# A two-layer decoder on one core: a gating unit's v product as one seven-product scheme, its layer norm's g and b moved behind the token mixing, and four weight residuals by accumulating transfers

## The chip, the cores and the metric

The kernel runs on one core of a Trainium2 chip. A core has engines with an instruction queue each: TensorE (PE in the profile; its weight loads are PEld), VectorE (DVE), ScalarE (ACT), GpSimd (POOL) and SyncE (SP), which here only issues transfers. They share an on-chip memory of 128 partitions and wait for each other by semaphores; matmul results stand in PSUM, in banks of 128 x 512 float32. The metric is the device time of one execution in microseconds, the median of several runs.

## The reference

x is 512 tokens of D = 1024 float32 values, and there are two layers. Each layer has a mixer and an MLP, each behind an RMS norm whose output is modulated by columns of `silu(c) @ ada_w` (48 columns of 128 for each layer, called modulation columns here). Layer 0's mixer is a pooling one, layer 1's is the gating unit that this change is about.

```python
h = modulate(rmsnorm(x, norm_mix_g[i]), sh1, sc1)
x = x + g1 * mixer(h)                       # i = 0: pooling; i = 1: sgu_mixer
h = modulate(rmsnorm(x, norm_mlp_g[i]), sh2, sc2)
x = x + g2 * (square(relu(h @ w1)) @ w2)    # D -> 4096 -> D

def sgu_mixer(h, w_in, ln_g, ln_b, w_s, b_s, w_out):
    z = gelu(h @ w_in)                      # 1024 -> 2048, exact gelu
    u, v = split(z, 2, axis=-1)
    v = layernorm(v, ln_g, ln_b)            # over 1024 features, eps 1e-5
    v = v.reshape(B, 4, 128, 8, 128)        # 4 chunks of 128 tokens, 8 heads of 128
    ws = where(tril(128, 128), w_s, 0)      # w_s: 8 x 128 x 128
    mixed = einsum('hts,bnshc->bnthc', ws, v) + b_s.T[None, None, :, :, None]
    return (u * mixed.reshape(B, 512, 1024)) @ w_out
```

## The kernel before

**Products in parts.** Every float32 operand of a product is split into a high part that TensorE takes in one pass and a residual: a weight tile `raw` gives `wh` (a copy by ACT) and `wl` (raw minus wh, by DVE), activations give `hb`/`op`/`as`/`gt` in the same two parts. A product is then three matmuls into one bank, wl x high, wh x residual and wh x high (`mm3`). `split` does this for a 128 x 1024 weight tile:

```python
A.activation(h[:, c], r[:, c], AF.Copy)
V.tensor_tensor(l[:, c], r[:, c], f32(h[:, c]), ALU.subtract)
```

**Stages, by time in the profiled execution.** Start, pooling mixer and the first sweep of MLP 0 to about 87 us; the rest of MLP 0 to 361; the gating unit from 361.4 to about 490; MLP 1 to about 797; the last norm and the store. Both MLP matrices already go through a seven-product scheme (Strassen's, in Winograd's form: block sums of weights and operands, seven block products for eight). Sums of weight blocks (`bt`, `tr`, `yr`) are partly made by transfers that accumulate into a tile, issued by POOL.

**Gating unit.** v has token rows on the partitions: for two halves of its columns (`ch`) and two halves of the tokens (`hf`), 8 feature blocks by 2 token tiles by 3 matmuls of 512 columns, then `Gelu` out of PSUM. `normed` meanwhile makes the second token half of h. The layer norm takes mean and variance of each token tile on DVE, the power for 1/sqrt on POOL (`rr<-rv`), scales v (`v<-v,ag,rr`), and applies `lnt`, which holds g and b for all partitions, by two DVE operations (`v<-v,lnt`). u is made with features on the partitions, 8 blocks `u0` to `u7` of 8 feature blocks x 3 matmuls. A mix `m0` to `m7` (one head) is 4 matmuls of v against the masked, transposed w_s in `wb[:, 0]`; DVE adds the bias in `wb[:, 1]` (`po<-po,wsbs`), multiplies by u (`u<-po,u`), ACT copies the high part and DVE makes the residual (`gt<-u,gt`). This one line orders u blocks and mixes:

```python
for op in "u0 u1 u2 u3 m0 u4 m1 m2 u5 m3 m4 u6 m5 u7 m6 m7".split():
```

The output projection takes `gt` against w_o in two column halves (`dh`) of four weight tiles each, four token tiles each; the first three token tiles take the heads 0 to 5 first and 6 and 7 afterwards. `gated` adds the result to x.

**Buffers.** PSUM is two pools of four banks: `xz` (v, mixes, projection) and `ps` (u, transposes, MLP parts). Weight parts `wh`/`wl` have five pairs. Three `raw` buffers of 128 x 1024 (pool `w4`) hold both raw weights and the modulation columns' tiles `ada`, each of which takes one DVE operation (`ada<-ada,cb`). `gq` has eight buffers of 128 x 2048 (tag g); `hx` holds single large tiles. `shift(pool, n)` puts an unused pad of n bytes a partition ahead of a pool's next tiles.

**Order.** The code after `plan.on = True` does not issue instructions: `Plan` records them and a list scheduler orders them for each engine, by a table of costs, by latest times counted back from PE's order, and by `yields`, by which DVE and ACT leave work that is not urgent for later. PE's order is that of the code. All instructions so issued bear line 128; code ahead of it bears line 100.

## Time and profile before

| | |
|---|---|
| time, median of 3 runs | 804.65 us (803.54 to 805.01) |
| profiled execution: its own time / span | 807.26 us / 805.2 us |
| granted TensorE clock, mean over the span | 0.997 |
| PE busy / PEld busy | 786.2 us (98%) / 712.0 us (88%) |
| DVE / ACT / POOL busy | 685.8 us (85%) / 504.9 us (63%) / 83.6 us (10%) |
| transfers | 183.35 MB, mean 228 GB/s |
| share of the chain that ended last | PE 79%, DMA 9%, DVE 5%, issue 4%, ACT 2% |

A row of groups reads "line engine operation out<-in partitions x elements xcount | busy us, mean ns of one | idle us before them, and what ended it". A row of the timeline reads "start, duration, engine, line, operation" and in brackets a wait and its releaser. A window's row has its length, the busy time of each engine with the instructions in it, the granted clock, the share of the transfer engines and GB/s. Matmuls overlap one another, so one's duration is longer than its share of TensorE's time, which is read from the distance of starts.

### The profile page before, as it was taken

The numbers are of one execution on the slowest core, as the hardware profiler recorded it, in microseconds if no ns is written. First come the engines' busy times: TensorE is split into PE (matmuls) and PEld (weight loads), VectorE is DVE, ScalarE is ACT, GpSimd is POOL, SyncE is SP. The second block draws the span as 40 slices with busy tenths as digits, with TensorE's granted clock in tenths as the row PEclk, the third lists the DMA queues.
The fourth block names the chain that finished last, engine by engine and source line by source line (L and its number), as shares of the span: only waits on it lengthen the run. The fifth ranks groups of instructions, "written<-read, shape, count | busy, mean of one in ns | idle before, by whom it ended". The sixth has DMA issues, their size and how long they took to land.

```text
span 805.2 us, 12574 instructions
## 1 busy us (share of the span) xinstructions
PE 786.2 (98%) x4868; PEld 712.0 (88%) x4868; DVE 685.8 (85%) x888; ACT 504.9 (63%) x718; POOL 83.6 (10%) x110
## 2 busy tenths in 40 slices
PE   5999999999999999999999999999999999999996
PEld 5678889999988888888889889999999998888885
DVE  5989799999789997986798878888778678998896
ACT  5486687777766666866234236777767685666672
POOL 4000001000010131010020002010000011112100
PEclk9999999999999999999999999999999999999998
DMA  8988958897999999244745756378776789999802
GB/s 342 417 303 298 358 195 286 272 281 209 312 291 241 232 242 257 95 161 140 256 154 205 260 195 213 143 199 241 228 235 172 183 261 272 199 230 208 216 14 91
DMA packets 46955, 183.35 MB, mean 228 GB/s; under 512 B 5272, under 2 KB 5424, under 8 KB 42928
## 3 DMA queue, kind: packets, MB, share of 16 engines
q1 hardware_dynamic: 36432, 129.33, 43.9%
q0 software_dynamic: 10032, 50.87, 30.5%
q10 hardware_dynamic: 432, 2.36, 0.7%
q8 instruction: 38, 0.62, 0.3%
q14 instruction: 21, 0.17, 0.1%
HBM read 176.23 MB, written 6.30 MB: 227 GB/s over the span
## 4 chain that ended last, share of the span: by engine, by line
PE 79%; DMA 9%; DVE 5%; issue 4%; ACT 2%; SPq 0%; POOLq 0%; POOL 0%; DVEq 0%; ACTq 0%
PE po L128 40%; PE pm L128 36%; DMA ada<-in_ada 3%; DMA raw<-in_w 1%; DMA wh<-in_ada 1%; DVE wl L128 1%; DMA bt<-in_w 1%; DMA x<-in_xtok 1%; ACT wh L128 1%; DVE ada L100 1%; PE po L100 1%; DMA yr<-in_w1b 1%; DMA tr<-in_w1b 1%; PE pq L100 0%; PE px L128 0%
## 5 line engine op out<-in xcount | busy, mean ns | idle before, releaser
L128 PE MATMUL pm<-wh,op 128*128 128x512 f32 x896 | 267.5, 379 | 0.0
L128 PE MATMUL po<-hb,wh 128*128 128x256 f32 (+1 forms) x1104 | 211.3, 295 | 0.0
L128 PEld LDWEIGHTS pm<-wh,op 128*128 128x128 f32 x896 | 169.4, 189 | 24.0
L128 PEld LDWEIGHTS po<-hb,wh 128*128 128x128 f32 x1104 | 174.2, 191 | 5.5
L128 PE MATMUL pm<-wl,op 128*128 128x512 f32 x448 | 169.9, 379 | 0.4 <-DVE wl L128 0.4
L128 PE MATMUL po<-hb,wl 128*128 128x256 f32 (+1 forms) x553 | 160.9, 296 | 0.9 <-ACT g L128 0.9
L128 PEld LDWEIGHTS po<-hb,wl 128*128 128x128 f32 x553 | 104.6, 191 | 4.1 <-ACT g L128 1.1
L128 PE MATMUL po<-as,wh 128*128 128x256 f32 x576 | 97.2, 275 | 0.0
L128 ACT ACTIVATE op<-g 128x1024 fp32r<-128x1024 f32 x56 | 59.1, 1061 | 58.5 <-PE pm L128 46.3
L128 PEld LDWEIGHTS pm<-wl,op 128*128 128x128 f32 x448 | 84.7, 189 | 12.5 <-DVE wl L128 0.7
L128 DVE TENSOR_TENSOR op<-g,op 128x1024 fp32r<-128x1024 f32 x56 | 68.1, 1220 | 24.0 <-ACT op L128 24.0
L128 PEld LDWEIGHTS po<-as,wh 128*128 128x128 f32 x576 | 87.4, 192 | 0.0
L128 DVE TENSOR_TENSOR wl<-bt,wh 128x1024 fp32r<-128x1024 f32 x64 | 76.8, 1217 | 7.1 <-ACT wh L128 7.1
L128 PE MATMUL po<-as,wl 128*128 128x256 f32 x288 | 79.3, 275 | 0.6 <-ACT g L128 0.6
L128 ACT ACTIVATE wh<-bt 128x1024 fp32r<-128x1024 f32 x64 | 67.4, 1053 | 19.8 <-PE pm L128 14.9
L128 ACT ACTIVATE wh<-tr 128x1024 fp32r<-128x1024 f32 x48 | 50.9, 1060 | 36.3 <-PE po L128 17.5
L128 DVE TENSOR_TENSOR wl<-raw,wh 128x1024 fp32r<-128x1024 f32 (+1 forms) x52 | 60.6, 1176 | 14.4 <-ACT wh L128 14.4
L128 DVE SCALAR_TENSOR_TENSOR ada<-ada,cb 128x1024 f32<-128x1024 f32 x56 | 67.9, 1217 | 5.1 <-DMA ada<-in_ada 5.1
L128 ACT ACTIVATE g<-g 128x512 f32<-128x512 f32 x100 | 61.8, 628 | 16.3 <-DVE g L128 15.1
L128 ACT ACTIVATE wh<-raw 128x1024 fp32r<-128x1024 f32 (+1 forms) x52 | 51.6, 1004 | 28.5 <-PE po L128 11.9
L128 DVE TENSOR_TENSOR wl<-tr,wh 128x1024 fp32r<-128x1024 f32 x48 | 58.6, 1221 | 10.8 <-ACT wh L128 10.7
L128 PEld LDWEIGHTS po<-as,wl 128*128 128x128 f32 x288 | 55.3, 192 | 0.8 <-ACT g L128 0.8
(192 smaller groups left out, 1135.1 us busy)
## 6 DMA issues: line engine op xcount, KB each, us to landing
ada<-in_ada SPq DMA_DIRECT2D x76, 512.0 KB, 4.9
bt<-in_w POOLq DMA_DIRECT2D x22, 1024.0 KB, 9.7
yr<-in_w1b SPq DMA_DIRECT2D x22, 512.0 KB, 6.4
bt<-in_w SPq DMA_DIRECT2D x16, 512.0 KB, 7.6
b<-in_w SPq DMA_DIRECT2D x16, 512.0 KB, 9.7
raw<-in_w SPq DMA_DIRECT2D x13, 512.0 KB, 6.8
tr<-in_w1b SPq DMA_DIRECT2D x12, 512.0 KB, 6.8
raw<-in_w1b SPq DMA_DIRECT2D x12, 512.0 KB, 5.3
```

The source lines that it names most:

```text
L100: return f(*a, **kw)
L128: self.ops.append((name, attr, lambda: f(*a, **kw), out, ins, kw))
```

## The change

**v's product.** The h @ w_v product is cut into 2 x 2 x 2 blocks (256 tokens, 512 features, 512 columns) and made as seven products v1 to v7, each 4 feature blocks x 2 token tiles x 3 matmuls of 512 columns. Partial sums that several results share stay in PSUM (`VX`, `VZ`); others go to v by ACT (copies) and are joined there by DVE (`v<-v,po`). Operand sums are made on DVE from a float32 copy of h (`hq`, which `normed` now fills in place of the scratch tile `tt`) and split again (`hs`). Weight sums are built in one tile `vb`: POOL issues 1 MB transfers that accumulate a further block into it, after the splits of the product before have read it.

```diff
+    CHAIN_ = {5: (0, 1), 6: (1, 1), 4: (1, 0)}
+    def h_sum(m):
+        if m == 5:
+            V.tensor_tensor(ha(1, 1), ha(1, 0), ha(1, 1), ALU.subtract)
+            t_[7] = get_gb().rearrange("p (k c) -> p k c", k=4)
+            V.tensor_tensor(t_[7], ha(0, 0), ha(1, 0), ALU.subtract)
...
+    def v_prep(m):
...
+        w = [split_d(b[q], src and wv_at(*src, q)) if f"v{m}{q}" in LO else split(b[q]) for q in range(2)]
+        if m in (1, 5, 6):
+            G.dma_start(whole_(VB[0, 0, 0]), wv_at(*CHAIN_[{1: 5, 5: 6, 6: 4}[m]]), accum_op=ALU.add)
+        if m == 5:
+            v_load(1, 1)
+        elif m == 3:
+            v_load(0, 1)
+            G.dma_start(whole_(VB[0, 1, 0]), wv_at(1, 1), accum_op=ALU.add)
...
+    def v_run(m, w):
+        banks = VX if m in (1, 6, 7, 4) else VS if m == 2 else VZ
...
+            if m in (1, 5) or m in (6, 3) and "v" not in half_:
+                A.activation(o, po, AF.Copy, scale=-1.0 if m == 6 else 1.0)
...
+            if m in (2, 3):
+                V.tensor_tensor(o, o, po, ALU.add)
+            elif m in (7, 6):
+                V.tensor_tensor(o, o, po, ALU.subtract)
+            A.activation(o, po if m == 4 else o, AF.Gelu)
```

**g and b.** v is only centred and scaled. g is a factor of a mix's row, applied together with the bias by one operation; b times the masked row sums of w_s is added to the bias table once. The row sums take a mask on POOL, a reduction on DVE, a transpose on PE and two transfers by POOL, out to memory and back to all partitions.

```diff
-        for n, op in ((0, ALU.mult), (1, ALU.add)):
-            V.tensor_tensor(v, v, lnt[:, n].rearrange("p (a b) -> p a b", a=2), op)
+    def rows():
...
+        G.affine_select(out=w, in_=w, compare_op=ALU.is_ge, fill=0.0, base=0, pattern=[[0, HEADS], [-1, P]], channel_multiplier=1)
+        V.tensor_reduce(rs, w, mybir.AxisListType.X, ALU.add)
+    def spread_rows(rs):
...
+        G.dma_start(line, r)
+        G.dma_start(b, line.rearrange("(o k) p -> o (k p)", o=1).to_broadcast([P, D]))
+        for h in range(HEADS):
+            V.scalar_tensor_tensor(wb[:, 1, h], b[:, P * h : P * h + P], vec[:, V_LNB + h : V_LNB + h + 1], wb[:, 1, h], ALU.mult, ALU.add)
     def do_mix(hd):
-        V.tensor_tensor(p4, p4, wb[:, 1, hd, :].unsqueeze(1).to_broadcast([P, 4, P]), ALU.add)
+        V.scalar_tensor_tensor(p4, p4, vec[:, V_LNG + hd : V_LNG + hd + 1], wb[:, 1, hd, :].unsqueeze(1).to_broadcast([P, 4, P]), ALU.mult, ALU.add)
```

**Residuals by transfers.** For u5, u7 and the third and fourth weight tile of the projection's first half, `wl` is no DVE subtraction: ACT writes minus the high part, and POOL issues a transfer that adds the raw weights from memory.

```diff
+    LO = "u5 u7 o2 o3".split()
+    def split_d(r, src=None):
+        h, l = wpair()
+        A.activation(h, r, AF.Copy)
+        A.activation(l, r, AF.Copy, scale=-1.0)
+        G.dma_start(l, r if src is None else src, accum_op=ALU.add)
```

**Order.** One line orders all of it: v products, u blocks (u0 and u1 in token halves, so that they can start before the second half of h is there), mixes `m`, their gates `g` (product with u and the parts), norms `n`, and modulation columns `c`. Each product's weights are prepared one product ahead.

```diff
-    for op in "u0 u1 u2 u3 m0 u4 m1 m2 u5 m3 m4 u6 m5 u7 m6 m7".split():
+    SEQ = "v1 v2 u0a u1a r0 u0b v5 u1b c2 u2 v6 c2 v3 c2 r1 v7 c2 u3 c1 n0 n1 v4 c1 n2 n3 c1 u4 c1 u5 m0 u6 m1 m2 c1 m3 g0 g1 u7 m4 g2 s0 g3 m5 m6 m7 g4 g5 g6 g7".split()
-    shift(hx, BASE)
+    shift(vy, BASE)
+        lock = {i for i, o in enumerate(ops) if o[0] == "POOL" and o[1] == "tensor_tensor"}
+        gap = {i for i in lock if any(ops[j][0] == "DVE" for j in succs[i])}
```

In the planner, `lock` lets POOL's element operations (the powers) be placed only where DVE is free, and `gap`, of 2.0 us, holds DVE back shortly before such a power that DVE awaits. A pad moves from the pool `hx` to the pool `vy`, which shifts the places of the tiles allotted behind it.

POOL's queue in the gating unit, before (-) and after (+); `rr<-sums` are the powers of RMS norms and `rr<-rv` those of v's norm:

```order
 L128 DMA x_1266<-xd_930 128x2048
-L128 TENSOR_TENSOR rr<-sums,mhalf 128x1 x3
+L128 AFFINE_SELECT ada<-ada 128x1024
+L128 TENSOR_TENSOR rr<-sums,mhalf 128x1 x2
+L128 DMA vb<-in_w_v 128x2x1024
 L128 AFFINE_SELECT wsbs<-wsbs 128x1024
-L128 TENSOR_TENSOR rr<-sums,mhalf 128x1
+L128 TENSOR_TENSOR rr<-sums,mhalf 128x1 x2
+L128 DMA vb<-in_w_v 128x2x1024 x3
+L128 DMA rowsum<-line 8x128
+L128 DMA ada<-rowsum 128x1024
+L128 DMA wl<-in_w_u 128x1024
```

Ahead of the second mask now stands the mask of the row sums, and between the norms' powers stand four 1 MB issues, the row sums' two and the first residual transfer.

VectorE before, from m6's bias to the last residual and the columns behind it, where the projection begins:

```order
L128 TENSOR_TENSOR po<-po,wsbs 128x512
L128 SCALAR_TENSOR_TENSOR ada,pmv<-ada,cb 128x1024
L128 TENSOR_TENSOR u<-po,u 128x512
L128 TENSOR_TENSOR po<-po,wsbs 128x512
L128 SCALAR_TENSOR_TENSOR ada,pmv<-ada,cb 128x1024
L128 TENSOR_TENSOR u<-po,u 128x512
L128 TENSOR_TENSOR gt<-u,gt 128x512
L128 SCALAR_TENSOR_TENSOR ada,pmv<-ada,cb 128x1024
L128 TENSOR_TENSOR gt<-u,gt 128x512
L128 SCALAR_TENSOR_TENSOR ada,pmv<-ada,cb 128x1024 x2
```

Here biases, products with u and columns stand in turn. VectorE after, from m4's bias on; the products with u in it are those of heads 4, 5, 6 and 7:

```order
L128 SCALAR_TENSOR_TENSOR po<-po,vec,wsbs 128x512
L128 TENSOR_TENSOR gt<-u,gt 128x512
L128 TENSOR_TENSOR u<-po,u 128x512
L128 SCALAR_TENSOR_TENSOR po<-po,vec,wsbs 128x512
L128 TENSOR_TENSOR gt<-u,gt 128x512
L128 TENSOR_TENSOR u<-po,u 128x512
L128 TENSOR_TENSOR gt<-u,gt 128x512 x3
L128 SCALAR_TENSOR_TENSOR ada,pmv<-ada,cb 128x1024 x3
L128 SCALAR_TENSOR_TENSOR po<-po,vec,wsbs 128x512 x2
L128 TENSOR_TENSOR u<-po,u 128x512
L128 TENSOR_TENSOR mods_90<-pmv,vec 128x2
L128 TENSOR_TENSOR u<-po,u 128x512
```

Three columns now stand between the residual of head 5 and the biases of m6 and m7. On PE, u7 stands ahead of m4, and m5, m6 and m7 follow each other with the projection right behind them.

More of the change, by code (lines that the diff above doesn't have):

```diff
@@ L332, in run @@
                 for e in ready:
+                    if e == "DVE" and any(i in gap and when[i] <= now + 1e-9 and k - cost[i][1] < now + lead["gap"] for k, i in ready["POOL"]):
+                        continue
                     if free[e] > now + 1e-9 or e == "SP" and sum(x[0] for x in lines[e]) > self.QUEUED or len(lines[e]) > 6:
@@ L340, in run @@
                             k, i = heapq.heappop(ready[e])
-                            if when[i] <= now + 1e-9 and fits(i) and not (e in ("DVE", "ACT") and yields(e, i)):
+                            if when[i] <= now + 1e-9 and fits(i) and not (e in ("DVE", "ACT") and yields(e, i)) and not (i in lock and free["DVE"] > now + 1e-9):
                                 pick = i
@@ L369, in run @@
                         end = now + cost[i][1]
+                        if i in gap:
+                            free["DVE"] = now + cost[i][0]
                         heapq.heappush(events, (end, i))
@@ new lines, in decoder_kernel, with u_prep, u_run @@
+    wu, pu = {}, {}
+    def u_prep(n):
+        r = ur[:, n % 2]
+        Y.dma_start(r, w_u[n])
+        w = split_d(r, w_u[n]) if f"u{n}" in LO else split(r)
+        return [t.rearrange("p (k c) -> p k c", k=KD) for t in w]
+    def u_run(n, w, part=None):
+        if n not in pu:
+            pu[n] = bank("po")
+        po = pu[n]
+        c = ALL if part is None else slice(256 * part, 256 * part + 256)
+        for k in range(KD):
+            mm3(po[:, c], cut(w, ALL, k), apart(H(k, c)), k == 0, k == KD - 1)
+        if part == 0:
+            return
+        if n % 4 == 0 and n // 4 == len(us):
+            us.append(gq.tile([P, 4, S], F32, name="u", tag="g"))
+        x = us[n // 4][:, n % 4]
+        if part is None:
+            A.activation(in_row(x), in_turn(po), AF.Gelu)
+        else:
+            x, po = x.rearrange("p (r c) -> p r c", r=2), po.rearrange("p (r c) -> p r c", r=2)
+            A.activation(in_row(x), in_turn(po), AF.Gelu)
@@ L1585, in decoder_kernel @@
+    ex = cols
     h_[0] = hparts()
```

226 lines of the change are left out of this document (160 added, 66 removed).

## Prediction

> **What bounds the kernel now.** I read the busy times first, then the chain that ended last, then the gating unit's stretch by sub-stages.
>
> ```profile
> PE 786.2 (98%) x4868; PEld 712.0 (88%) x4868; DVE 685.8 (85%) x888; ACT 504.9 (63%) x718; POOL 83.6 (10%) x110
> PE 79%; DMA 9%; DVE 5%; issue 4%; ACT 2%; SPq 0%; POOLq 0%; POOL 0%; DVEq 0%; ACTq 0%
> ```
> PE is idle for 19 us of the 805.2 us span, nearly all of it at the two ends. VectorE comes next, with 119 us free. The windows below are v's product, u with the first mixes, the later mixes, and the output projection up to the next norm.
>
> ```profile
> core 0: us, PE busy (x) PEld busy (x) DVE busy (x) ACT busy (x) POOL busy (x), PEclk, DMA share, GB/s
> 361.40:404.70 43.30, 43.28 (x209) 37.82 (x208) 32.97 (x52) 19.57 (x28) 3.06 (x4) 1.00 0.60 203
> 404.70:425.50 20.80, 20.80 (x98) 18.13 (x97) 19.70 (x30) 6.73 (x10) 3.18 (x4) 1.00 0.47 158
> 425.50:453.60 28.10, 28.10 (x162) 25.50 (x162) 23.52 (x37) 11.47 (x16) 0.57 (x1) 1.00 0.62 226
> 453.60:489.84 36.24, 36.24 (x170) 31.68 (x170) 29.39 (x56) 11.96 (x23) 1.70 (x3) 1.00 0.64 218
> 361.40:489.84 128.44, 128.42 (x636) 113.13 (x635) 105.57 (x173) 49.73 (x76) 8.51 (x11) 1.00 0.59 205
> ```
> TensorE never waits here and its granted clock is 1.00, so a matmul taken away is time won. DVE has 128.44 - 105.57 = 22.9 us free, ACT 78.7 us. What the change adds to DVE must fit into 22.9 us, and at the right places.
>
> **The matmuls.** Matmuls overlap, so their price is the distance of starts, over one wl,wh,wh triple:
>
> ```profile
> 361.46 0.38 PE L128 MATMUL po<-wl,hb 128*128 128x512 f32 x1
> 362.11 0.38 PE L128 MATMUL po<-wl,hb 128*128 128x512 f32 x1
> ...
> 544.73 0.28 PE L128 MATMUL po<-as,wl 128*128 128x256 f32 x1
> 545.06 0.28 PE L128 MATMUL po<-as,wl 128*128 128x256 f32 x1
> ```
> That is 0.65/3 = 0.216 us for 512 columns and 0.33/3 = 0.111 us for 256. v had 2 halves x 8 feature blocks x 4 token tiles x 3 = 192 matmuls of 512 columns. It now has 7 products x 4 blocks x 2 token tiles x 3 = 168. 24 x 0.216 = **-5.2 us**. Two of the eight u products are cut into token halves: 96 matmuls of 256 columns for 48 of 512, 96 x 0.111 - 48 x 0.216 = **+0.3**. One more transpose (the row sums) is **+0.1**, by the 12 transposes in 1.31 us of the next row. Sum on TensorE: **-4.8 us**.
>
> ```profile
> 370.47 1.31 PE px L128 x12
> ```
>
> **VectorE.** Its prices:
>
> ```profile
> L128 DVE TENSOR_TENSOR wl<-ur,wh 128x1024 fp32r<-128x1024 f32 x8 | 9.7, 1217 | 0.0
> L128 DVE TENSOR_TENSOR xf<-xf 128x1024 f32<-128x1024 f32 x3 | 3.7, 1221 | 0.0
> L128 DVE TENSOR_TENSOR g<-g,po 128x512 f32<-128x512 f32 x24 | 16.3, 680 | 0.2 <-PE po L128 0.2
> L128 DVE TENSOR_TENSOR v<-v,lnt 128x1024 f32<-128x1024 f32 x8 | 9.4, 1215 | 0.0
> L128 DVE TENSOR_TENSOR po<-po,wsbs 128x512 f32<-128x512 f32 x8 | 5.6, 698 | 4.5 <-PE po L128 4.5
> L100 DVE SCALAR_TENSOR_TENSOR xf<-po,mg,xf 128x512 f32<-128x512 f32 x8 | 5.9, 750 | 1.0 <-PE po L100 0.8
> L100 DVE TENSOR_SCALAR diag<-ident,rr 128x128 f32<-128x128 f32 x2 | 0.5, 284 | 1.1 <-POOL rr L100 1.1
> L128 ACT ACTIVATE wh<-bt 128x1024 fp32r<-128x1024 f32 x64 | 67.4, 1053 | 19.8 <-PE pm L128 14.9 <-DMA bt<-in_w 4.8
> ```
> Weight residuals: 14 halves for v instead of 8, less the four that go by transfer, +2 x 1.2 = +2.4. Four operand residuals, of the same form, +4.8. Four sums of h blocks +4.9. Six adds of a product into v +4.1. Eight 128-wide bias updates, between nothing and the 0.28 of a 128-wide operation: 8 x 0.2 = +1.6. g now rides in the mix's bias add, at most 0.750 - 0.698 more, +0.4. g and b on v go: -9.4. Sum **+8.8 us**; the row-sum reduction, at most 1.2, comes before the stretch. 22.9 us free become 22.9 - 8.8 - 4.8 = 9.3: DVE does not become the bound, but its slack more than halves. ACT gains 21 instructions of at most 1.05 us (last row), under 22.1 against 78.7 free: nothing, unless one stands ahead of a split that PE awaits.
>
> **Where PE will wait, 1: the start of the output projection.** Before, u6 and u7 lay between the mixes. Now m4 to m7 come in a row and the projection follows; mixes and projection share four PSUM banks, so token tile 2 needs m6's bank, which its multiplication by u frees. The queue of VectorE from m4's end to that point (shown with the change) holds 12 operations of 512 columns and three modulation columns:
>
> ```profile
> 363.13 0.68 DVE L128 TENSOR_TENSOR tmp<-pm,gb 128x512 f32<-128x512 f32 x1
> 363.73 0.68 DVE L128 TENSOR_TENSOR hb<-tt,hb 128x512 fp32r<-128x512 f32 x1
> ...
> 453.28 0.70 DVE L128 TENSOR_TENSOR po<-po,wsbs 128x512 f32<-128x512 f32 x1
> 453.88 1.22 DVE L128 SCALAR_TENSOR_TENSOR ada<-ada,cb 128x1024 f32<-128x1024 f32 x1
> 455.02 0.08 DVE L128 DVE_READ_ACCUMULATOR ada<-ada,cb 128x1 f32 x1
> ```
> By distances of starts, 0.60 (363.13 to 363.73) and 1.14 for a column (453.88 to 455.02), that is 12 x 0.60 + 3 x 1.14 = 10.6 us, and some 0.2 to start. PE has m5 to m7 (3 x 8 matmuls of 0.11, 2.7) and the 36 matmuls of tiles 0 and 1 (7.8): 10.5. The wait is 0.3, or up to 0.7 if the biases cost what the row of 0.750 us says; I take **+0.7**, the nearest row.
>
> **Where PE will wait, 2: the projection's second half.** Its weights come through three raw buffers that the modulation columns free, one DVE operation each:
>
> ```profile
> 461.76 1.23 DVE L128 SCALAR_TENSOR_TENSOR ada<-ada,cb 128x1024 f32<-128x1024 f32 x1 [0.22 <-DMA ada<-in_ada]
> 465.24 1.23 DVE L128 TENSOR_TENSOR wl<-raw,wh 128x1024 fp32r<-128x1024 f32 x1 [1.82 <-ACT wh L128]
> 471.54 1.23 DVE L128 TENSOR_TENSOR wl<-raw,wh 128x1024 fp32r<-128x1024 f32 x1 [0.90 <-ACT wh L128]
> 473.11 2.36 DVE L128 TENSOR_TENSOR wl<-raw,wh 128x1024 fp32r<-128x1024 f32 x2 [0.34 <-ACT wh L128]
> ```
> Before, the last residual was done at 475.5 and wanted at 453.6 + (96 + 18) x 0.216 = 478.2: 2.7 us to spare, with DVE waiting 0.22 + 1.82 + 0.90 + 0.34 = 3.3 us on the way. Now DVE has, from m4's end, 9 x 0.60 + 3 x 1.14 = 8.8 us up to m6's bias and then, by its order (11 of 512, 5 columns, 4 residuals, some small ones), about 17 up to the last residual: 25.8. PE wants it after 2.7 + 0.7 + 114 x 0.216 = 28.0. With the old 3.3 us of waits PE loses 25.8 + 3.3 - 28.0 = 1.1; with none, nothing. But from the last column, which frees the last buffer, DVE has 4.9 us of work to the last residual, while the load (4.1) and ACT's copy (1.05) take 5.2:
>
> ```profile
> raw<-in_w_o SPq DMA_DIRECT2D x8, 512.0 KB, 4.1
> ```
> The last split is 0.3 later for that, 1.4 in all; the three ahead of it can each lose 0.2 more, together 2.0; with the DVE waits of before doubled it is 1.1 + 3.3 = 4.4. I take **+2.0**, since the columns now stand right ahead of these splits.
>
> **The new transfers.** Accumulating ones of 1 MB, a plain load of 512 KB, and, last, the spread of the landings of the accumulating ones:
>
> ```profile
> bt<-in_w POOLq DMA_DIRECT2D x22, 1024.0 KB, 9.7
> ur<-in_w_u SPq DMA_DIRECT2D x8, 512.0 KB, 4.7
> DMA to landing us min/median/max: 4.3/9.2/14.8
> ```
> From v5's second split to v6's weights: 9.7 + 1.05 (ACT) + 1.2 (DVE) = 12 us, in which PE has v5, half of u1 and u2: 60 x 0.216 = 13.0. v7's weights can be loaded only when v5 has freed a buffer: 4.7 + 9.7 + 2.3 = 16.7 us, in which PE has half of u1, u2, v6 and v3: 84 x 0.216 = 18.1. Cost 0, with margins of 1.0 and 1.4. With landings of 14.8 they would cost 4.1 and 3.7. The residuals of u5, u7 and two blocks of the projection are half as large and are issued around the powers of v's norm, two products (48 x 0.216 = 10.4) or more before PE needs them: 0, at the 9.7 of the 1 MB ones too. On POOL the row sums' round trip and these issues stand ahead of the powers for v's norm; from v4's end to the first mix PE has u4 and u5, 10.4 us, against statistics, power and scaling of some 5: 0.
>
> [...]
>
> **POOL and the order elsewhere.** A mask on POOL beside a residual on DVE:
>
> ```profile
> 360.62 1.51 POOL L128 TENSOR_SCALAR_AFFINE_SELECT wsbs<-wsbs 128x1024 f32<-128x1024 f32 x1 [1.06 <-DMA wsbs<-in_wsT]
> 361.09 2.12 DVE L128 TENSOR_TENSOR wl<-raw,wh 128x1024 fp32r<-128x1024 f32 x1
> ```
> 2.12 instead of 1.22: the mask held DVE for 0.9 us. There is one mask more, ahead of the gating unit, in the stretch of this row:
>
> ```profile
> 300.00:361.40 61.40, 61.40 (x294) 53.95 (x293) 52.97 (x62) 42.85 (x58) 7.35 (x10) 1.00 0.59 173
> ```
> DVE has 61.40 - 52.97 = 8.4 us idle there: 0. The planner's new rule for POOL's powers adds no instruction; it moves rows from 340 us to the end. In the second MLP splits and operand residuals now alternate, PE's queue is unchanged. What PE's first products waited for DVE in the whole trace:
>
> ```profile
> L128 PE MATMUL pm<-wl,op 128*128 128x512 f32 x448 | 169.9, 379 | 0.4 <-DVE wl L128 0.4
> ```
> With 0.4 us in 448 products there is room: 0, at worst 1. The moved pad changes tile addresses, and the 1024-wide rows above read 1215 to 1221 ns for three different tiles: 0.
>
> **Sum.** -4.8 + 0.7 + 2.0 = **-2.1 us**. The profiled execution took 807.26 us (span 805.2), so it would take 805.2; the median of the runs is 804.65, so I predict **802.5 us**.
>
> **Rivals.**
> A. *The waits don't come.* DVE keeps 9.3 us free, and if it runs ahead of PE both places cost nothing: -4.8, 799.9 us. For it: before, it waited 4.5 us for PE at the bias adds. Against: the order puts three columns ahead of m6's bias.
> B. *The waits eat the gain.* Sums over DVE hide that it stood at 19.70 of 20.80 us ahead of the first mixes. If it arrives there 1 to 3 us later than I reckon, each of these places and v's norm hands that on: 3.2 to 6.4 us of waits, 803.1 to 806.2.
> C. *Slower: accumulating transfers land late.* One mechanism: v5's, v6's and v7's weights hang on 1 MB landings. From about 10.7 (v6) and 11.1 us (v7) on PE waits; at 14.8 it loses 7.8, and -2.1 + 7.8 gives +5.7, 810. It decides from 13 us on. Against: the load on the transfer engines is 0.60 here.
> D. *The change does not do what it says*: PE would have as many matmuls as before, +2.7 by the waits alone. The order shows 168 where 192 stood: no chance.
>
> **How the numbers follow.** The measurement tells 0.2% (1.6 us) from nothing: faster is under 803.0, slower over 806.3. The forecast, waits of 1 to 3.2 us, 0.34; A 0.18; B 0.33; C and a still later DVE 0.15. So faster 0.52, same 0.33, slower 0.15. The likeliest case's own range is 800.9 to 803.1. Half the spread of the runs shown (803.54 to 805.01) is 0.7; the range goes that far beyond A's and B's ends, 799.2 to 806.9, and leaves out most of C.
>
> **What would show it.** The page after: PE some 5 us less busy, and its idle time longer by the waits. PE starts po<-wh,gt rows late, waiting for DVE u and for wl or ACT wh in the projection: right if about 0.7 and 2. DVE busy about 694 us. No PE wait at po<-w,hs (v5, v6, v3, v7): right for the transfers; a wait there on wh<-vb shows C. I am wrong if PE waits in the first products, before the mixes, or in the second MLP, or if DVE's 512-wide operations stop overlapping.

## The result and the profile after

| | before | after |
|---|---|---|
| median, each of 6 runs on one chip | 804.69 us | 809.56 us (806.09 to 810.57) |
| ratio, with its 95% interval | | 1.0058 [1.0038, 1.0077] |
| profiled execution: its own time / span | 807.26 / 805.2 us | 810.57 / 808.8 us |

The change makes the kernel 4.9 us slower; 2.1 us faster was forecast. The page of after, busy times, shares of the chain that ended last, and two rows of its list of transfers (name, queue, count, size, median us from issue to landing):

```profile
PE 785.4 (97%) x4893; PEld 710.4 (88%) x4893; DVE 695.1 (86%) x905; ACT 520.6 (64%) x739; POOL 106.0 (13%) x121
...
PE 69%; DMA 11%; DVE 9%; issue 5%; ACT 4%; SPq 1%; POOLq 0%; POOL 0%; ACTq 0%; DVEq 0%
...
bt<-in_w POOLq DMA_DIRECT2D x22, 1024.0 KB, 9.5
...
vb<-in_w_v POOLq DMA_DIRECT2D x4, 1024.0 KB, 12.7
```

PE has lost ten points of the chain, DVE, transfers and ACT have won eight. The last row points to the reason: v's four accumulating transfers take 12.7 us to land in the median, while their siblings of the same kind and size, `bt`, take 9.5 (9.7 before).

Stretches of after with the prediction's columns: from v's start to the projection's start, the projection with what follows up to MLP 1, and v6 with v3:

```profile
361.12:453.42 92.30, 90.06 (x492) 79.96 (x491) 77.05 (x123) 53.63 (x75) 16.78 (x18) 0.98 0.81 229
453.42:500.03 46.61, 44.32 (x211) 37.36 (x209) 41.25 (x80) 18.45 (x35) 2.64 (x4) 1.00 0.78 261
396.66:409.85 13.19, 12.41 (x48) 10.25 (x49) 8.85 (x11) 7.95 (x11) 2.39 (x2) 0.87 0.87 186
```

And before, cut at the same places of the program:

```profile
361.03:453.33 92.30, 92.28 (x467) 81.53 (x466) 76.28 (x119) 38.13 (x54) 7.18 (x8) 1.00 0.58 200
453.33:496.39 43.06, 43.06 (x210) 37.89 (x209) 35.62 (x70) 17.43 (x33) 1.70 (x3) 1.00 0.63 213
```

The first stretch lasts 92.30 us in both, though it has less work for PE after. In after PE stands idle 92.30 - 90.06 = 2.24 us in it, and the clock is 0.98: inside the 90.06 us is a stretch at half clock (granted 0.50 from 398.24 to 401.64 us). The transfer engines are busy 0.81 of the time instead of 0.58. The second stretch is 3.55 us longer. Both MLP 1 sweeps and the tail together take 308.83 us before and 308.81 after, so all of the loss is in these two rows.

What PE waited for in after (total us, times, longest):

```profile
PE po L128 <- DVE wl L128: 2.3, 3, 0.8
PE po L128 <- ACT wh L128: 1.2, 2, 1.0
...
PE po L128 <- DVE mods L128: 0.6, 1, 0.6
```

PE's timeline at the start of v6:

```profile
395.03 0.59 PE L128 MATMUL po<-hb,wh 128*128 128x512 f32 x2
396.66 0.48 PE L128 MATMUL po<-wh,hs 128*128 128x512 f32 x1 [1.03 <-ACT wh L128]
397.92 0.51 PE L128 MATMUL po<-wl,hs 128*128 128x512 f32 x1 [0.78 <-DVE wl L128]
398.24 1.05 PE L128 MATMUL po<-wh,hs 128*128 128x512 f32 x2
...
401.64 0.39 PE L128 MATMUL po<-wl,hs 128*128 128x512 f32 x1
401.87 0.59 PE L128 MATMUL po<-wh,hs 128*128 128x512 f32 x2
```

v6's first matmul waits 1.03 us for ACT's high part, the second 0.78 for the residual. Then, from 398.2 to 401.6, two matmuls take 1.05 us where two take 0.59 before and after that: 3.41 us at a granted clock of 0.50, 1.7 us lost. The chain that ended last, across that place:

```profile
383.88 11.64 DMA vb<-in_w_v
395.55 1.06 ACT wh L128
396.64 1.24 DVE wl L128
397.92 12.10 PE po L128 x47
```

Read upwards: PE waits for DVE's residual, that for ACT's copy, that for a transfer of 11.64 us. The transfer also goes out late against PE:

```profile
382.35 0.45 PE L128 MATMUL po<-wh,hs 128*128 128x512 f32 x1 [0.20 <-DVE hs L128]
...
382.11 1.23 DVE L128 TENSOR_TENSOR wl<-vb,wh 128x1024 fp32r<-128x1024 f32 x1
...
383.88 1.21 POOL L128 DMA_DIRECT2D vb<-in_w_v  x1 [17.40 <-DVE wl L128]
```

PE begins v5 at 382.35, but v5's second split, which must have read `vb` before the transfer writes it, is done only at 383.34, and POOL issues 0.5 us later. From that split to v6's residual at 397.88 pass 14.5 us, while PE has matmuls up to 395.46, that is 12.1 us. On ACT the same transfer holds up more than the copy:

```profile
395.55 3.90 ACT L128 ACTIVATE wh<-vb 128x1024 fp32r<-128x1024 f32 x4 [3.69 <-DMA vb<-in_w_v]
399.36 1.06 ACT L128 ACTIVATE u<-po 128x512 f32<-128x512 f32 x2
```

ACT stands 3.69 us ahead of the four copies, then works on them for 3.90, and the `Gelu`s of u1 and u2, whose matmuls PE had done by 390.5 and 395.6 us, come behind them at 399.36.

The projection of after, with its two remaining kinds of wait:

```profile
462.03 0.45 PE L128 MATMUL po<-wh,gt 128*128 128x512 f32 x1 [0.56 <-DVE mods L128]
...
476.73 0.48 PE L128 MATMUL po<-wh,gt 128*128 128x512 f32 x1 [0.18 <-ACT wh L128]
477.99 0.48 PE L128 MATMUL po<-wl,gt 128*128 128x512 f32 x1 [0.78 <-DVE wl L128]
...
481.77 0.48 PE L128 MATMUL po<-wl,gt 128*128 128x512 f32 x1 [0.78 <-DVE wl L128]
```

**The account**, from v's first matmul to the end. PE idles 1.03 + 0.78 = 1.81 us at v6 and 0.43 in two other places (for DVE's `hb` and `hs`), 2.24. Half clock takes 1.7. Of its busy time another 1.05 goes to the four restarts, 0.26 each: a matmul behind a wait is counted with some 0.48 us, where one in a row takes 0.216. Together 4.99: without it the stretch would be 87.31 us, which a run below shows by itself, and which is 4.99 below before's. In the projection 2.30 of waits and the restarts make most of the 3.55. So -4.99 + 4.99 + 3.55 = +3.6, as in the spans. The medians differ by 4.9; the other 1.3 lies within what single executions differ by (before's profiled one is 2.6 us above its median), and no trace settles it. Each trace is of one execution, which can lie off its kernel's median: of the runs below e3's took 817.33 us (median 810.66), e5's 803.92 (806.15) and e14's 802.59 (804.17).

### The profile page after: what moved, and what is told of

Same layout as the page of the kernel before. It is cut to its first block, busy times and chain, and to the rows that moved or that the text cites. A ratio compares the mean times of both kernels' runs of the same rounds, so it can differ in the third digit from the quotient of the medians.

```text
span 808.8 us, 12689 instructions
## 1 busy us (share of the span) xinstructions
PE 785.4 (97%) x4893; PEld 710.4 (88%) x4893; DVE 695.1 (86%) x905; ACT 520.6 (64%) x739; POOL 106.0 (13%) x121
## 4 chain that ended last, share of the span: by engine, by line
PE 69%; DMA 11%; DVE 9%; issue 5%; ACT 4%; SPq 1%; POOLq 0%; POOL 0%; ACTq 0%; DVEq 0%
PE po L128 35%; PE pm L128 29%; DMA vb<-in_w_v 3%; DVE wl L128 3%; DMA ada<-in_ada 2%; ACT wh L128 2%; DMA bt<-in_w 2%; PE po L100 2%; PE px L100 1%; DMA raw<-in_w 1%; DMA x<-in_xtok 1%; ACT g L128 1%; DMA raw<-in_w_o 1%; PE pq L100 1%; DVE ada L100 1%
## 5 line engine op out<-in xcount | busy, mean ns | idle before, releaser
L128 PEld LDWEIGHTS po<-hb,wh 128*128 128x128 f32 x1136 | 177.8, 192 | 5.1 <-DVE hb L128 0.4
L128 PE MATMUL po<-hb,wl 128*128 128x256 f32 (+1 forms) x569 | 163.4, 292 | 0.0
L128 PEld LDWEIGHTS po<-hb,wl 128*128 128x128 f32 x569 | 107.7, 192 | 2.9 <-DVE wl L128 0.4
L128 DVE TENSOR_TENSOR wl<-raw,wh 128x1024 fp32r<-128x1024 f32 (+1 forms) x44 | 50.2, 1150 | 11.9 <-ACT wh L128 11.9
L128 ACT ACTIVATE wh<-raw 128x1024 fp32r<-128x1024 f32 (+1 forms) x46 | 45.4, 998 | 22.1 <-DMA raw<-in_w_o 10.2
```

The source lines that it names most:

```text
L128: self.ops.append((name, attr, lambda: f(*a, **kw), out, ins, kw))
```

## The experiments

All kernels are after with the edit shown. The theory: **late landings** (v's 1 MB transfers land after PE wants their weights, at a place where the transfer engines are loaded) plus, apart from it, **the projection's DVE order**. Rivals: the half clock alone, ACT's order, DVE's work, the planner's rule for POOL, the transfers for residuals. Ratios are to the kernel before on the same chip.

### The place: half clock, order of u3, two halves, v as before

e1: work that depends on nothing stands ahead of v6, so that PE does not idle there.

```diff
+            if x == "v6":
+                d_ = bank("pb")
+                for _ in range(12):
+                    T.matmul(d_[:, 0:P], ones, ones, start=True, stop=True)
```

> The changed kernel with 12 idle matmuls (ones by ones, 128 columns, into a bank that nobody reads) put ahead of v6 in PE's order. Theory 1 (the wait at v6, 1.0 us for wh and 0.8 us for wl, drops TensorE's clock to a half for 3.4 us, which costs 1.7 us more): the fill covers the first wait, the wait for wl stays, no half-clock stretch around v6, mean granted clock 0.997 or more, 1.5 to 2 us faster than the changed kernel (some 808). Rival (the clock drop has nothing to do with PE's idle time, or is not what costs): the clock drops all the same and the time is the same or up to 1.3 us longer.

Measured 811.98 us, 1.0090 [1.0077, 1.0103]. v6 with v3:

```profile
397.76:408.20 10.44, 10.44 (x51) 9.07 (x50) 6.87 (x10) 5.12 (x8) 0.94 (x1) 1.00 1.02 210
```

10.44 us at clock 1.00 instead of 13.19 at 0.87: without the waits there is no half clock here. That fits the theory but does not show it, since in e6, e7 and e9 the same two waits at v6 bring no half clock either. And the fill itself waited 1.48 us for a bank that u's late `Gelu` held, 1.7 us went at the first mix, and the projection took 47.1 us: the first stretch is 94.11 us, 1.8 longer than in after. Filling the gap gains nothing: what PE waits for is still late.

e2: u3 goes ahead of v6, 5.2 us more work before it.

```diff
-    SEQ = "... u2 v6 c2 v3 c2 r1 v7 c2 u3 c1 n0 n1 v4 ..."
+    SEQ = "... u2 u3 v6 c2 v3 c2 r1 v7 c2 c1 n0 n1 v4 ..."
```

> The changed kernel with u3 moved from behind v7 to ahead of v6, so that PE has 24 matmuls (5.2 us) more while v6's weight sum is on its way. Theory 1 (the 1 MB accumulating transfer for v6 lands 1.9 us too late, and the half clock follows from it): no wait at v6, no half clock, 3.5 to 4 us faster than the changed kernel, 805.5 to 806. Theory 2 (VectorE is too full in the whole gating unit, v6 is only where it shows): the wait comes back at v3, v7 or v4 with 1 us or more, and the time stays within 1 us of the changed kernel, 809.

814.27 us, 1.0118 [1.0103, 1.0132]. v6 no longer waits, but u3 waits 1.5 us for a `Gelu` that stands behind v6's copies on ACT, and v4, now right behind v7, waits for a bank:

```profile
418.70 0.45 PE L128 MATMUL po<-wh,hb 128*128 128x512 f32 x1 [3.61 <-DVE v L128]
```

Half clock follows, 3.41 us of it. u3 is now missed between v7 and v4, and the wait has only moved.

e3: v6's transfer (and v5's and v4's) in two halves, each with its own landing.

```diff
-            G.dma_start(whole_(VB[0, 0, 0]), wv_at(*CHAIN_[...]), accum_op=ALU.add)
+            for q in range(2):
+                G.dma_start(VB[0, 0][q], wv_at(*CHAIN_[...], q), accum_op=ALU.add)
```

> The changed kernel with each of the three accumulating 1 MB transfers of the chain v1-v5-v6-v4 issued as two of 512 KB, the first as soon as the first split has read its half. Theory 1 (the landing of the 1 MB piece is the wait): v6's weights come 2 us or more earlier, the wait and the half clock go, 3 to 4 us faster than the changed kernel, some 806. Rival (the transfer engines are shared, so the last byte lands at the same time): the second half lands as late as before, the wait stays near 1.8 us and the time at 809.

810.66 us, 1.0082 [1.0051, 1.0114]. v6's halves land in 5.8 and 7.1 us, the first is issued without waiting for v5's second split, and PE has no wait there: what it waited for at v6 was the transfer. The wait moves to v7, whose transfer stayed whole:

```profile
405.65 0.48 PE L128 MATMUL po<-wh,hs 128*128 128x512 f32 x1 [2.06 <-ACT wh L128]
```

6.83 us of half clock follow, and the first stretch, 93.95 us in this trace, is no shorter.

e4: v as before (192 matmuls, no sums), all other parts of the change kept.

```diff
-    SEQ = "v1 v2 u0a u1a r0 u0b v5 u1b c2 u2 v6 ..."
+    SEQ = "r0 u0 c2 u1 c2 r1 u2 c2 n0 n1 n2 n3 u3 c2 u4 c2 c1 u5 m0 u6 m1 ..."
```

> The changed kernel with v's product as before the change (192 matmuls, no block sums and no accumulating transfers for v); g and b behind the mixing, the four residual transfers, the order of mixes and projection and the planner's rules stay. Theory 1 (the 4.8 us of fewer matmuls are lost at v6 and before, and the projection's 3.4 us come from the new order of mixes, columns and transfers, whatever v is): 804.7 + 3 = 807 to 808.5, with the waits in the projection still there. Theory 2 (VectorE's extra work for the seven products makes the projection late): the projection's waits fall below 1 us and the time is 804 to 805.5.

806.09 us, 1.0017 [1.0008, 1.0027]: about 1.4 us above before. The two stretches:

```profile
358.24:451.88 93.64, 92.66 (x468) 81.52 (x467) 62.65 (x106) 41.34 (x58) 11.12 (x14) 1.00 0.64 200
451.88:495.35 43.47, 43.47 (x210) 37.76 (x209) 39.84 (x78) 18.09 (x34) 3.09 (x4) 1.00 0.81 276
```

g and b behind the mixes and the residuals by transfer cost 1.3 us in the first stretch, 1.0 of it one wait for `hb`, and the projection has no wait although DVE does nearly as much in it (39.84 us). So most of the 4.9 us comes with the v scheme, the projection's part too, which suggests that it depends on how far behind DVE is when the projection starts.

### What makes the landing late

e14 keeps the order of every engine and cuts the accumulating transfers to an eighth of their bytes (the planner is told the old size; v and four residuals are not the reference's).

```diff
-            G.dma_start(whole_(VB[0, 0, 0]), wv_at(...), accum_op=ALU.add)
+            G.dma_start(whole_(VB[0, 0, 0])[:, :, 0:P], wv_at(...)[:, :, 0:P], accum_op=ALU.add)
```

> The changed kernel, every engine in the same order, but each of its eight accumulating transfers for v, u and the projection moves an eighth of its columns (6 MB less in the gating unit; the rest of those tiles stays without its sum or residual). If late landings are the whole loss, their own and those that they cause beside them: no wait over 0.4 us at v6, v7, the mixes and in the projection, no half clock, and the 4.8 us of fewer matmuls appear: 799.5 to 801.5. If VectorE's added work is a loss of its own: the projection's waits of 2 to 3.4 us stay, 802.5 to 804.

804.17 us, 0.9988 [0.9977, 0.9999].

```profile
357.98:445.29 87.31, 87.31 (x493) 78.70 (x491) 77.06 (x123) 53.66 (x75) 17.46 (x18) 1.00 0.64 198
445.29:491.29 46.00, 44.12 (x210) 37.44 (x209) 41.05 (x80) 18.42 (x35) 2.63 (x4) 1.00 0.68 229
```

PE is busy for all of the first stretch, at full clock, with the same DVE, ACT and matmul work: the 4.99 us of the matmuls are there as soon as the bytes land in time. The projection keeps 2.94 of its 3.55 us, so that these bytes are not what it loses by; its four waits, 1.88 us, all end with DVE. Together the two stretches change by -4.99 + 2.94 = -2.05 us against before; of the whole time the ratio gives 1.0 us less, with an interval that ends just short of no change.

e12 leaves out one 512 KB load of u's weights (u4 then uses old weights), so that v6's transfer has less beside it.

```diff
-        Y.dma_start(r, w_u[n])
+        if n != 4:
+            Y.dma_start(r, w_u[n])
```

> The changed kernel without the load of u4's weights, which SP issues 0.6 us behind v6's accumulating transfer (u4 is then made with u2's weights, so 512 KB are left out). In the two traces the 26 accumulating 1 MB transfers landed the later the more was in flight beside them, some 8.5 us with 0.9 MB and 11 to 14 us with 2 MB. If that is what made v6 late: its transfer has 1.1 to 1.3 MB beside it instead of 1.6, lands in 9.5 to 10.8 us instead of 11.6, the two waits at v6 fall from 2.2 us together to about 1.0, and 1 to 3 us go from the time (3 where the half clock goes too). If the transfer takes 11 to 12 us by itself: landing, waits and time stay.

815.51 us, 1.0125 [1.0109, 1.0141]. The answer is in two rows of the timeline: issued at 382.00, v6's transfer lets ACT go on at 390.82, 8.8 us later instead of 11.6.

```profile
382.00 1.21 POOL L128 DMA_DIRECT2D vb<-in_w_v  x1 [17.12 <-DVE wl L128]
...
390.82 3.91 ACT L128 ACTIVATE wh<-vb 128x1024 fp32r<-128x1024 f32 x4 [1.99 <-DMA vb<-in_w_v]
```

v6's wait is gone. While the transfer was under way 0.75 MB moved beside it, against 1.63 in after (from the issue and landing times of all transfers, each counted by the share of its own time that overlaps). This does not show that the amount is the cause: the count grows with the landing time itself, and the edit took out 0.5 MB of the 0.88, the planner's other order the rest. Nor is it how busy the transfer engines are, and that half of the theory falls. `bt`'s transfers, whose median of 9.7 us the forecast took, run in before where these engines are busy all the time (0.99 from 650 to 735 us, and here), against 0.81 in v's stretch of after:

```profile
213.99:297.41 83.42, 83.42 (x400) 73.28 (x400) 79.73 (x79) 55.45 (x61) 12.70 (x16) 1.00 1.00 254
```

What separates the kernels is when SP issues the next load of u's weights (u4's in after). In after, e1, e2, e6, e7 and e9 it comes 0.62 us behind v6's transfer, which lands in 11.6 to 11.7 us. In e8, e15 and e17 it comes 1.8 to 2.0 us behind, in e12 not at all, and v6's transfer lands in 8.8 to 9.9. After's load, and e8's transfer, load and landing:

```profile
384.50 0.33 SPq L128 DMA_DIRECT2D ur<-in_w_u  x1
...
381.72 1.19 POOL L128 DMA_DIRECT2D vb<-in_w_v  x1 [15.26 <-DVE wl L128]
...
383.53 0.33 SPq L128 DMA_DIRECT2D ur<-in_w_u  x1
...
391.62 1.07 ACT L128 ACTIVATE wh<-vb 128x1024 fp32r<-128x1024 f32 x1 [1.90 <-DMA vb<-in_w_v]
```

By the packet records of the traces, v6's first packet starts 3.8 to 4.0 us after the issue in the first six kernels and 1.9 in the other four. So a load issued right behind seems to get ahead of the transfer. The four differ from after in other ways too, and no run moves that load alone: this is a strong hint and not shown. The kernel as a whole got slower, since the planner made other orders of it: waits at v7 and in the mixes.

e8 takes away the planner's rule for POOL's powers.

```diff
-        lock = {i for i, o in enumerate(ops) if o[0] == "POOL" and o[1] == "tensor_tensor"}
+        lock = set()
```

> The changed kernel without the planner's new rule for POOL's powers (it may place them beside VectorE again). My sum put this rule at 0: within 0.7 us of the changed kernel's 809, with powers that take 1 us or more beside VectorE and some that hold a scaling up. If the rule matters, for or against: 2 us or more either way, by PE waits at the transposes of the norms or at m0.

818.32 us, 1.0172 [1.0157, 1.0186]. PE waits 6.4 us at v7, for a transfer that took 15.4. The rule was priced at 0 in the prediction; without it the order that comes out is worse by 8.8 us, and why was not found.

### The projection

e7 makes the four residuals on DVE again.

```diff
-    LO = "u5 u7 o2 o3".split()
+    LO = "".split()
```

> The changed kernel with the four weight residuals (u5, u7 and two tiles of the projection) made by VectorE again, no accumulating transfers for them: 4 x 1.2 = 4.8 us more on VectorE, 2 MB less by transfers. Theory 2 (VectorE full): the projection's and the mixes' waits grow by 2 to 5 us, 811 to 814. Rival (the projection is late because columns and gains wait behind the residual transfers, which land in 8 to 10 us): loads of the columns at the projection land in 4 to 5 us instead of 7 to 8, the waits there fall, 806 to 808.

809.73 us, 1.0060 [1.0048, 1.0072]: no change against after, and in neither range. v to projection 90.84 us (the waits at v6 are there, but no half clock: granted 1.00 over the stretch), projection 48.34, where PE waits 2.9 us for `gt`: with the residuals to make, DVE is later there.

e6 takes mixes and gates apart (`m4 g3 s0 m5 g4 u7 m6 g5 m7 g6 g7` for `u7 m4 g2 s0 g3 m5 m6 m7 g4 ...`).

> The changed kernel with only the order behind v4 changed: m1 to m4 right behind m0 and u6, u7 between m5 and m6, and each gate one mix behind its own, so that PE has u7's 24 matmuls while VectorE does gates. If the projection is late because biases, gates and three columns stand together ahead of it: its waits fall from 2.3 us to under 1 and the time by 1.5 to 2.5 us against the changed kernel. If it is late because VectorE arrives there with a backlog from the seven products: waits of the same size come back at the mixes or the projection, and the time is within 1 us of the changed kernel's 809.

808.89 us, 1.0053 [1.0040, 1.0066]. The bank wait of 0.56 goes; the projection still takes 47.29 us, since PE now waits 1.4 us for `wl<-in_w_o` there and 1.8 in three smaller waits.

e9 hands the projection's modulation columns out later: one behind each token tile of its first half instead of two, and seven in its second half instead of three.

```diff
-                for _ in range(2):
+                for _ in range((1, 1, 1, 1, 4, 3, 0, 0)[4 * dh + t]):
```

> The changed kernel with eleven modulation columns of the projection handed out later: one behind each token tile of its first half and seven in its second half, where there were eight and three; by its order VectorE now has the biases and products of m5 to m7 ahead of all these columns. If the projection is late because VectorE reaches it with a backlog, and columns stand ahead of gates and of the raw buffers: the projection falls from 46.6 us to 44 or less (43.1 before the change), nothing else moves, 2 to 3 us faster than the changed kernel. If the second half waits for w_o's loads for another reason (transfers that land late): the waits for wh and wl stay, within 1 us of 46.6.

821.12 us, 1.0189 [1.0166, 1.0212].

```profile
465.13 0.77 PE L128 MATMUL po<-wl,gt 128*128 128x512 f32 x1 [9.00 <-DMA wl<-in_w_o]
```

PE waits 9.0 us for a residual transfer; half clock begins 3.9 us into this wait and lasts 10.2, 5.2 of them after it. POOL issued the residual transfers at 454.3 and 456.3, after waits of 1.09 and 1.15 us for ACT's `wl`, and they landed 10.7 and 12.5 us later, while PE wanted the first at 456.1: the long landings did most of it.

### Versions meant to be faster

e5: all four transfers in halves (e3's edit for v7 too), u3 ahead of v7, and gates between the mixes:

```diff
-    SEQ = "... r1 v7 c2 u3 c1 n0 n1 v4 c1 n2 n3 c1 u4 c1 u5 m0 u6 m1 m2 c1 m3 g0 g1 u7 m4 g2 s0 g3 m5 m6 m7 g4 ..."
+    SEQ = "... r1 u3 v7 c2 c1 u4 n0 n1 v4 c1 n2 n3 c1 u5 c1 u6 m0 m1 g0 m2 c1 g1 m3 g2 s0 u7 m4 g3 m5 m6 m7 g4 ..."
```

> The changed kernel with all four accumulating 1 MB transfers as two of 512 KB each, u3 between v3 and v7, u4 between v7 and v4, and so u5 and u6 between v4 and the first mix, u7 between m3 and m4. Theory 1, as it now stands (the weight sums of v6 and v7 land too late for PE and each wait brings a half-clock stretch; with halves alone the wait had moved to v7): no PE wait over 0.3 us and no half clock from v1 to the first mix, where PE then takes some 70 us instead of 74.7; the projection's waits stay near 3 us; 804 to 806. Theory 2 (VectorE is too full): the waits move on to the mixes and the projection, which lose 2 us or more beyond the changed kernel's, and the time stays at 808 or above.

806.15 us over 12 runs, 1.0016 [1.0002, 1.0029]: 3.4 us of the loss are back.

```profile
359.71:448.21 88.50, 87.83 (x493) 78.80 (x491) 77.51 (x122) 53.46 (x75) 19.84 (x22) 1.00 0.84 238
448.21:494.38 46.17, 43.59 (x210) 37.70 (x209) 40.62 (x80) 17.72 (x34) 2.60 (x3) 1.00 0.77 260
...
461.86 0.48 PE L128 MATMUL po<-wh,gt 128*128 128x512 f32 x1 [1.75 <-DVE gt L128]
```

v1 to v4 run without a wait, with the same bytes and the engines at 0.84: smaller pieces and a product of room are together enough for the transfers. The projection keeps 3.1 us of loss.

e10 is e5 with e9's edit, e11 that with e6's order of mixes, e13 e5 with the columns spread otherwise:

```diff
+    SEQ = "... v3 c2 c1 r1 u3 v7 c2 u4 n0 n1 v4 n2 n3 u5 u6 m0 m1 c1 g0 m2 c1 g1 m3 c1 g2 s0 u7 m4 g3 m5 m6 m7 g4 ..."
+                for _ in range((2, 1, 1, 1, 4, 3, 0, 0)[4 * dh + t]):
```

> The kernel of the two halves with room (all accumulating 1 MB transfers as two halves, u3 ahead of v7, u4 ahead of v4) with the columns handed out later. Both causes taken away: no wait over 0.5 us from v1 to the first mix, projection 44 us or less instead of 46.2, so 806.2 - 2.5 = 803.5, the first kernel of these with a time under that of before (804.6). If the waits only move on: 805.5 to 807.

> As the kernel with all three, but m4 and m5 ahead of u7 and m6, m7 behind it, so that PE has u7's 5.2 us while VectorE does the gates of heads 3 and 4. If VectorE's backlog at the projection's start still costs PE: 0.5 to 1.5 us faster than the kernel with all three. If the columns alone made it: the same within 0.5 us.

> Halves, u3 ahead of v7, u4 ahead of v4, and the columns taken away from v's norm and from the projection's start: one more behind v3, three between the mixes, two behind the first token tile of the projection and one behind the next three, seven in the second half. If late transfers, the half clock and VectorE's queue at three places (v's norm, the projection's start, w_o's second half) are the whole loss: no wait over 1 us in the gating unit, some 131 us from v1's start to the end of the projection (135.4 before the change, 137.1 for the kernel of halves with room), 801 to 804. If other waits come in their place: 805 or more.

e10 806.34 us, 1.0023 [1.0008, 1.0039]; e11 813.65, 1.0120 [1.0099, 1.0141], with 6.6 us of waiting for `wl<-in_w_o`; e13 805.54, 1.0015 [1.0002, 1.0027]. In e10 and e13 PE no longer waits at the projection's weights; it waits at the first mix (1.5 and 2.62 us, for v) and at the next norm's transposes (1.9 and 2.3, for `xs`). In e13, on DVE and on PE:

```profile
429.27 1.23 DVE L128 SCALAR_TENSOR_TENSOR ada<-ada,cb 128x1024 f32<-128x1024 f32 x1 [5.18 <-DMA ada<-in_ada]
430.43 1.28 DVE L128 BATCH_NORM_STATS2 stt<-v 128x6 f32<-128x512 f32 x2
...
436.63 0.46 PE L128 MATMUL po<-wsbs,v 128*128 128x128 f32 x2 [2.62 <-DVE v L128]
```

DVE stands 5.18 us before a column whose load is not there; the statistics of v behind it are ready to run and are what the first mix waits for.

e15 tells the planner that accumulating transfers take longer; e16 is e5 with that; e17 and e18 are the same two with the new cost for `vb` and `wl` only.

```diff
-            t = (5.2 if kw.get("accum_op") else 4.0 if ... else 2.6) * mb
+            t = (8.0 if kw.get("accum_op") else 4.0 if ... else 2.6) * mb
```

> The changed kernel with one number of the planner's cost table changed: an accumulating transfer costs 8.0 us a MB instead of 5.2, so that a 1 MB one is planned to land in 11 us instead of 8.2. PE's order stays; VectorE, ACT, SP and POOL are ordered anew, in the MLPs too. If in-order queues that wait for landings which the plan had earlier are what passes lateness on: fewer waits behind late loads, 804 to 807. If transfers are late whatever stands around them: 808 to 811.

> The kernel of halves with room (u3 ahead of v7, u4 ahead of v4, 512 KB halves) with the planner's 8.0 us a MB. If room and a plan that knows how late transfers land are both needed: 802 to 804.5, under the kernel before. If the plan alone decides: as the run with the costs alone. If new waits come: 806 or more.

> The changed kernel with the planner's 8.0 us a MB for accumulating transfers into v's weight sums and into the residuals alone; those of the MLPs keep 5.2, so that start and MLPs are ordered as before. If the 35 us of the run with the costs alone came from the MLPs: start and MLPs as in the changed kernel, and only the gating unit differs, 804 to 810. If a plan with later landings is worse here too: over 811.

> Halves with room, and the planner's 8.0 us a MB for the gating unit's accumulating transfers alone. If queues that were planned on early landings hold the rest of the gain: 133 us or less from v1's start to the end of the projection (134.7 with halves and room, 135.4 before), 802 to 805, under the kernel before. If not: 806 or more.

e15 844.50 us, 1.0493 [1.0473, 1.0514]; e16 845.64, 1.0501 [1.0472, 1.0529]; e17 812.42, 1.0117 [1.0071, 1.0163]; e18 812.52, 1.0103 [1.0078, 1.0127]. The longer cost made every kernel slower by its median. With it everywhere the rest of the kernel comes in a worse order too (in e15 v starts at 373.3 us instead of 361.3 in after, and what follows the projection is 15 us longer), and with it only here the first stretch does get shorter (e17 88.87 us, e18 87.61) while the projection takes 50.1 and 49.9. No version with the whole computation beats the kernel before.

## Why the prediction was wrong, by its steps

- **The matmuls, -4.8: right.** e14 shows -4.99, with nothing else in the way.
- **The new transfers, "Cost 0, with margins of 1.0 and 1.4": this step failed.** For v6 it reckoned 12 us from v5's second split to the weights, and 13.0 us of matmuls for PE meanwhile. After shows 14.5 and 12.1: the landing took 11.64 instead of the median's 9.7, the issue took 0.5 that had no term, and PE began v5 1.0 us before that split was done, which alone uses up the margin of 1.0. So PE waited 1.81 us; the half clock behind the waits, 1.7, and the restarts, 1.05, had no price in the sum at all. With 0.43 of waits for `hb` and `hs`, which e14 does not have either, that makes the 4.99 us of v's stretch. Rival C, at 0.15, had the mechanism and the place; but it "decides from 13 us on", and 11.64 was enough, and the 0.60 of load that spoke against it decides nothing (`bt`'s 9.7 come from stretches at 0.99 and 1.00). For v7 the margin held: PE did not wait there.
- **The projection, 0.7 + 2.0 = 2.7: right in kind and nearly in size.** The bank wait is 0.56, the waits for the second half 0.18 + 0.78 + 0.78 = 1.74; the stretch is 3.55 longer, 2.94 of it without the bytes of the new transfers. The restarts were left out here too. That e14's two stretches give -2.05, the forecast's -2.1, is in part luck: the matmuls are 0.2 better than reckoned and the projection 0.24 worse. What in DVE's order makes these waits is argued from e4 and e14; the runs that move columns or gates (e6, e9, e10, e13) only moved the waits, so that this stays open. Rival A, no waits, is refuted; rival B's later mixes did not come.
- **VectorE, +8.8: right in size.** Its busy time in the two stretches is 77.05 + 41.25 against 76.28 + 35.62, +6.4. But one modulation column (1.2) now stands ahead of them, and before's includes the 0.9 by which the mask lengthened a residual: like for like about +8.5. On the page it is 695.1, where 694 was forecast. The prices that had no row before, measured in after:

```profile
L128 DVE SCALAR_TENSOR_TENSOR po<-po,vec,wsbs 128x512 f32<-128x512 f32 x8 | 5.9, 757 | 2.0 <-PE po L128 2.0
...
L128 DVE TENSOR_TENSOR v<-v,po 128x512 f32<-128x512 f32 x6 | 3.9, 684 | 0.0
L128 DVE TENSOR_TENSOR hq<-hq 128x1024 f32<-128x1024 f32 x3 | 3.7, 1228 | 0.0
...
L128 DVE SCALAR_TENSOR_TENSOR wsbs<-ada,vec,wsbs 128x128 f32<-128x128 f32 x8 | 2.2, 356 | 0.0
```

  The mix's factor costs 0.757 - 0.698 = 0.06 each, just above its bound of 0.05. The 128-wide bias update is 0.356 by itself and 2.2 / 8 = 0.28 in a row, at the upper end of what was allowed: 2.2 where 1.6 was taken. 8 h sums and residuals at 1.23 agree.
- **ACT, 0 "unless one stands ahead of a split that PE awaits": the exception came the other way round.** The splits, waiting for their transfer, stood ahead of `Gelu`s that PE awaited (e1, e2).
- **MLP 1 and the pad, 0: right**, 308.83 against 308.81 us. **The planner's rule, 0: not shown**; without it e8 is 8.8 us slower than after.
- **The page after:** PE "some 5 us less busy" was 0.8 less, since matmuls at half clock (3.40 of 3.40 us from 398.24 to 401.64) and the restarts count as busy, in the projection too. "No PE wait at po<-w,hs" was the forecast that told the transfers apart, and the wait there is the one that showed the step false.

## What to carry to other kernels

A landing time taken from a median said little of one transfer here (9.5 to 13.9 us for v's four, against 9.7): reckon from the moment at which it can be issued to the moment at which PE wants its data, look which load is issued right behind it (its effect is a hint here, not shown), and demand the margin from the slow siblings. Issue in halves what is wanted in halves (v6's landed in 5.8 and 7.1 us, the whole in 11.64). A wait of PE cost more than its length here: about 0.26 us of restart for each of the four in after's first stretch, and 1.7 us of half clock behind the two at v6. ACT stood 3.69 us for v6's late transfer, and u's `Gelu`s behind its copies were late with them, so what the copies hold up must be priced with the copies.

## What was not expected of the hardware

- **Busy transfer engines alone did not make an accumulating transfer late.** v's four 1 MB transfers took 9.5 to 13.9 us where these engines were busy 0.81, their 22 siblings `bt` 9.7 in the median where they were busy all the time (0.99 and 1.00 in before). And bytes on POOL's queue, where the accumulating transfers are (q0), held the transfer engines longer than those on SP's (q1); queue, packets, MB, share of the 16 engines' span:

```profile
q1 hardware_dynamic: 36432, 128.81, 43.0%
q0 software_dynamic: 11872, 57.69, 35.0%
```

  Of the span of 808.8 us that is 2.7 us of all 16 engines for 1 MB on q1 and 4.9 on q0. v's stretch of after has 6.19 MB on q0, where before has 0.53, and 14.91 instead of 17.87 on q1: so 15% more GB/s (229 against 200) became 40% more load (0.81 against 0.58).
- **Half clock after two short waits.** In the gating unit stretches of 3.41 us (after, e2), 6.83 (e3) and 10.2 (e9) were read, each at or behind a PE wait of 1 us or more (1.03, 3.61, 2.06 and 9.00). In after 1.03 and 0.78 us of idling, 1.26 us apart, brought one; in e6, e7 and e9 the same waits brought none (granted clock of the first stretch 1.00 in e6 and e7). What decides between the two is not shown.
- **A small POOL operation beside DVE.** A power of the RMS norm ahead of the gating unit, 128 x 1, took 12.43 us in after (0.93 before), while DVE ran operations with two inputs from 340.19 to 352.98 without a gap:

```profile
340.35 12.43 POOL L128 TENSOR_TENSOR rr<-sums,mhalf 128x1 f32<-128x1 f32 x1 [4.09 <-DVE sums L128]
```

  Beside before's 0.93, at 338.65, DVE ran such operations too, from 338.48 to 340.90, so that what made this one long is not shown. PE did not wait for it here.
